# Two orders of the high and low matmuls in a stationary-weight projection

## The chip, the cores and the metric

The kernel runs on one core of one Trainium2 chip. Its time is the device time of one execution in microseconds (us); runs are compared by their medians. The core's engines each work through a queue of their own: TensorE (PE in the profile, its weight loads PEld), VectorE (DVE), ScalarE (ACT), GpSimd (POOL) and SyncE (SP, which issues the DMAs). They wait for each other by semaphores.

## What is computed

A trunk of two layers on 256 tokens of width 2048, all in float32. Layer 0 mixes tokens by differential attention (8 heads, q and k normed, partial rotary), layer 1 by a Mamba-2 state-space mixer (8 groups). Each is followed by an MLP with a squared ReLU of width 8192, and each of the four stages begins with an RMS norm.

```python
for i in range(DEPTH):
    hn = rms_norm(h, mixer_norm[i])
    mix = diff_attention(hn, ...) if i % 2 == 0 else mamba2_mixer(hn, ...)
    h = h + mix
    h = h + sq_relu_mlp(rms_norm(h, mlp_norm[i]), mlp_w1[i], mlp_w2[i])

def sq_relu_mlp(h, w1, w2):
    return jnp.square(jax.nn.relu(h @ w1)) @ w2
```

Nearly all of the work is the projections: q, k, v and o, the mixer's in and out, and the two matrices of each MLP.

## The kernel before

TensorE multiplies in a rounded float32 format (`float32r`), in one pass. To keep float32's precision, both operands are split in two: a high part, which is the value rounded to that format, and a low part, which is the rest. A product is then high x high + high x low + low x high.

Weights come from HBM in blocks of 128 partitions x 1024 columns (`load`, SP's queue, tile `raw`, four buffers). `split_weights` makes the two parts of a block in a tile `w` (four buffers): ACT casts `raw` to the high part `wh` (L158), and DVE subtracts that from `raw` for the low part `wl` (L159).

Two kinds of projection use such blocks. In `sub_block` the weights are stationary: a block holds eight k-tiles of 128 x 128, and each k-tile is loaded into the array and multiplied with 256 tokens of an activation. An activation tile holds its high part and its low part side by side, 256 columns each. So one matmul of the weight's high part takes all 512 columns (L168) and leaves high x high in the left half of a PSUM bank and high x low in the right half. The matmul of the weight's low part takes the activation's high part alone, 256 columns (L172), and adds to the left half. `add_sums` adds the halves later on ACT and DVE (L205, L206). This text calls the 512-column matmul a high one and the 256-column matmul a low one. Before, a block does its eight highs and then its eight lows. Each has its own weight load. q and k (`wide_pair`), the state-space mixer's in-projection (`wide_pair`) and half of each MLP's first matrix (`wide_one`) go this way: 354 blocks in all.

In `token_block` the activations are stationary and the weights move, always 512 columns (L222, L224). `seven` does the other half of the MLP's first matrix by Strassen's scheme, also with 512 columns each (L536 to L538).

Everything smaller (norms, attention scores, rotary, convolution, the scan) is side work. It is written as generators that wait in two queues of `Side`; `side.tick()` lets the first one of each queue go a step further. The projections call `tick` at fixed places: `sub_block` three times in a block, after the fourth high, after the eighth, and after the last low. Where the next activation is not there yet, it ticks until it is. L130 (the norm's mean spread over partitions), L141 (column sums for a norm), L408 and L410 (scores and mask) and L774 (the scan) are matmuls of side work.

A scheduler of the framework then puts the instructions of each engine in order. Mostly it keeps the order of the code, but where it reckons with a wait it moves a later instruction ahead.

Of the kernel before, what the change touches and what calls it, by code (L numbers as in the profile page):

```python
# [20 lines left out]
P = 128  # L21
# [67 lines left out]
def trunk_kernel(ctx: ExitStack, tc: tile.TileContext, x, xt, par, rope, qk, wv, wo, w10, w10s, w20, win, wdt, wout, w11, w11s, w21, out):  # L89
    nc = tc.nc  # L90
    V, S, G, PE = nc.vector, nc.scalar, nc.gpsimd, nc.tensor
# [51 lines left out]
    side = Side()  # L143
# [18 lines left out]
    def sub_block(w, acts, k0, acc, start, stop):  # L162

        wh, wl = w
        for k in range(8):
            while len(acts) <= k0 + k:
                side.tick()
            PE.matmul(acc, lhsT=wh[:, k * P:(k + 1) * P], rhs=acts[k0 + k], start=(start and k == 0), stop=False)  # L168
            if k % 4 == 3:
                side.tick()  # L170
        for k in range(8):
            PE.matmul(acc[:, 0, :], lhsT=wl[:, k * P:(k + 1) * P], rhs=acts[k0 + k][:, 0, :], start=False, stop=(stop and k == 7))  # L172
        side.tick()

    def load(src, n=1):

# [9 lines left out]
    def wide_pair(src, b, acts):  # L186

        pp = [bank() for _ in range(2)]
        for s in range(2):
            raw = [load(src[b + t, s]) for t in range(2)]  # L190
            for t in range(2):
                sub_block(split_weights(raw[t]), acts, 8 * s, pp[t], s == 0, s == 1)
        return pp

    def wide_one(src, b, acts):
        pp = bank()
        raw = [load(src[b, s]) for s in range(2)]
        for s in range(2):
            sub_block(split_weights(raw[s]), acts, 8 * s, pp, s == 0, s == 1)
        return pp  # L200
# [101 lines left out]
    with tc.tile_pool(name="xin", bufs=1) as xp:  # L302
        xf = []
        for j in range(KT // 2):
            f = xp.tile([P, 2, T], F32, name=f"xf{j}")
            nc.sync.dma_start(out=f, in_=x[j])
            xf.append(f)
            if j in (0, 3, 5):
                raw.append(load(qk[len(raw) % 2, len(raw) // 2], 1 if j else 2))
        raw.append(load(qk[1, 1]))  # L310
        for j in range(4):
            nc.scalar.dma_start(out=h[:, :, cols(j)], in_=xt[:, :, cols(j)])
        for s in range(2):
            for j in range(4 * s, 4 * s + 4):
                xs += x_parts(xf[j], j, C_MIX0)
                if j == 4 * s:
                    w = split_weights(raw[2 * s], 1 if s else 2)
            for t in range(2):
                sub_block(w if t == 0 else split_weights(raw[2 * s + 1]), xs, 8 * s, first[t], s == 0, s == 1)
# [656 lines left out]
```

## Time and profile before

| | us |
|---|---|
| median of three runs | 2483.77 |
| the runs | 2481.91 to 2486.58 |
| the profiled execution, its own time | 2483.01 |
| its span, first to last instruction | 2481.3 |
| granted TensorE clock, mean | 1.000 |

The page gives for each engine the time that it was busy. Two groups that the change's neighbours belong to read as follows: the line in the code, the engine and operation, what is written and read, the count, then busy us and the mean ns of one, then idle time of the engine before them and what ended it.

```profile
L159 DVE TENSOR_TENSOR w<-raw,w 128x1024 fp32r<-128x1024 f32 (+1 forms) x739 | 896.3, 1220 | 344.8 <-ACT w L158 341.8
L158 ACT CAST w<-raw 128x1024 fp32r<-128x1024 f32 (+1 forms) x739 | 776.2, 1051 | 594.9 <-PE pp L222 451.6
L172 PEld LDWEIGHTS pp<-act,w 128*128 128x128 f32 x2832 | 384.7, 190 | 28.1 <-issue 1.7
```

A split of a block takes ACT 1051 ns and DVE 1220 ns. A weight load is recorded with 190 ns, beside the matmuls; loads overlap too, which is why 2832 of them are busy for 384.7 us only. The end of a matmul is modelled, so the distance between two starts says more than a duration. In the timeline, equal instructions that follow each other are merged into one row with a count: start, time from the first start to the last end, engine, line. The chain in order of time gives for each piece the time that it holds the end back.

### The profile page before, as it was taken

How to read it: one execution, taken by the hardware profiler on the slowest of the kernel's cores; microseconds unless marked ns; L12 is line 12 of the kernel's file. 1: busy time of each engine (PE TensorE's matmuls, PEld its weight loads, DVE VectorE, ACT ScalarE, POOL GpSimd, SP SyncE). 2: the span in 40 equal slices, each digit the busy share in tenths (PEclk: the TensorE clock that was granted, in tenths of full speed). 3: DMA queues.
4: the chain of work that ended last, by engine and by line, in shares of the span. 5: the costliest groups of instructions: out<-in, count | busy, mean ns of one | idle time of the engine just before them, and what ended most of it. 6: DMA issues, size and time to landing. Idle time of an engine off the chain costs nothing.

```text
span 2481.3 us, 33043 instructions
## 1 busy us (share of the span) xinstructions
PE 2456.4 (99%) x12462; PEld 2070.8 (83%) x12462; DVE 1967.4 (79%) x2558; ACT 1411.4 (57%) x2007; POOL 1.2 (0%) x8
## 2 busy tenths in 40 slices
PE   7999999999999999999999999999999999999999
PEld 6888887888888888888888888888788888888887
DVE  6788879977968949759886887887998696795874
ACT  6666656645545536556776576675565454554553
POOL 0000000000000000000000000000000000000000
PEclk9999999999999999999999999999999999999999
DMA  7445555465565555556555556455555556556554
GB/s 253 159 159 189 169 173 186 176 230 180 198 211 193 202 178 204 170 179 203 197 189 194 172 190 207 159 189 191 192 204 201 182 194 212 190 199 197 186 185 155
DMA packets 131120, 471.21 MB, mean 190 GB/s; under 512 B 14640, under 2 KB 14832, under 8 KB 130960
## 3 DMA queue, kind: packets, MB, share of 16 engines
q1 hardware_dynamic: 127152, 458.28, 54.8%
q10 hardware_dynamic: 3808, 10.81, 1.4%
q8 instruction: 98, 1.61, 0.3%
q14 instruction: 62, 0.51, 0.1%
HBM read 466.88 MB, written 2.16 MB: 189 GB/s over the span
## 4 chain that ended last, share of the span: by engine, by line
PE 96%; DVE 2%; DMA 1%; issue 0%; ACT 0%; ACTq 0%; SPq 0%; DVEq 0%
PE pp L222 27%; PE pp L168 26%; PE pp L172 14%; PE pp L224 13%; PE pp L536 4%; PE pp L537 4%; PE pp L538 4%; DVE w L159 1%; PE aux L774 1%; PE aux L576 1%; PE aux L141 0%; PE aux L408 0%; DMA raw<-in_w11s 0%; DMA h<-in_xt 0%; PE aux L268 0%
## 5 line engine op out<-in xcount | busy, mean ns | idle before, releaser
L159 DVE TENSOR_TENSOR w<-raw,w 128x1024 fp32r<-128x1024 f32 (+1 forms) x739 | 896.3, 1220 | 344.8 <-ACT w L158 341.8
L158 ACT CAST w<-raw 128x1024 fp32r<-128x1024 f32 (+1 forms) x739 | 776.2, 1051 | 594.9 <-PE pp L222 451.6
L222 PE MATMUL pp<-w,act 128*128 128x512 f32 x3072 | 962.7, 392 | 0.0
L168 PE MATMUL pp<-act,w 128*128 128x512 f32 x2832 | 721.7, 394 | 17.2 <-DVE act L250 13.0
L222 PEld LDWEIGHTS pp<-w,act 128*128 128x128 f32 x3072 | 574.7, 188 | 118.7 <-issue 2.1
L168 PEld LDWEIGHTS pp<-act,w 128*128 128x128 f32 x2832 | 511.5, 189 | 114.8 <-ACT w L158 17.9
L224 PE MATMUL pp<-w,act 128*128 128x512 f32 x1536 | 598.5, 390 | 0.0
L172 PEld LDWEIGHTS pp<-act,w 128*128 128x128 f32 x2832 | 384.7, 190 | 28.1 <-issue 1.7
L172 PE MATMUL pp<-act,w 128*128 128x256 f32 x2832 | 398.2, 283 | 0.0
L522 ACT CAST w<-raw 128x1024 fp32r<-128x1024 f32 (+1 forms) x256 | 241.3, 946 | 196.4 <-PE pp L172 111.0
L224 PEld LDWEIGHTS pp<-w,act 128*128 128x128 f32 x1536 | 288.6, 188 | 58.0
L523 DVE TENSOR_TENSOR w<-raw,w 128x1024 fp32r<-128x1024 f32 (+1 forms) x256 | 272.2, 1087 | 41.5 <-ACT w L522 38.5
L536 PE MATMUL pp<-w,sa 128*128 128x512 f32 x256 | 99.9, 390 | 0.0
L537 PE MATMUL pp<-w,sa 128*128 128x512 f32 x256 | 99.8, 390 | 0.0
L538 PE MATMUL pp<-w,sa 128*128 128x512 f32 x256 | 99.6, 389 | 0.0
L529 DVE TENSOR_TENSOR raw<-raw 128x1024 f32<-128x1024 f32 x64 | 78.1, 1221 | 6.8 <-DMA raw<-in_w10s 3.8
L537 PE MATMUL pp<-w,act 128*128 128x512 f32 x192 | 75.2, 391 | 0.0
L536 PE MATMUL pp<-w,act 128*128 128x512 f32 x192 | 75.1, 391 | 0.0
L538 PE MATMUL pp<-w,act 128*128 128x512 f32 x192 | 74.7, 389 | 0.0
L699 DVE SCALAR_TENSOR_TENSOR cy<-u,cwb,cy 128x256 f32<-128x256 f32 x144 | 62.9, 480 | 1.4
L205 ACT COPY relu<-pp 128x256 f32<-128x256 f32 x64 | 23.9, 373 | 63.9 <-PE pp L172 63.9
L536 PEld LDWEIGHTS pp<-w,sa 128*128 128x128 f32 x256 | 48.1, 188 | 10.5
(210 smaller groups left out, 1665.1 us busy)
## 6 DMA issues: line engine op xcount, KB each, us to landing
raw<-in_w SPq DMA_DIRECT2D x384, 512.0 KB, 3.9
raw<-in_win SPq DMA_DIRECT2D x160, 512.0 KB, 3.4
raw<-in_wout SPq DMA_DIRECT2D x64, 512.0 KB, 3.4
raw<-in_qk SPq DMA_DIRECT2D x63, 512.0 KB, 3.4
raw<-in_w10s SPq DMA_DIRECT2D x32, 768.0 KB, 4.4
raw<-in_w11s SPq DMA_DIRECT2D x32, 768.0 KB, 4.4
raw<-in_wv SPq DMA_DIRECT2D x32, 512.0 KB, 4.1
raw<-in_wo SPq DMA_DIRECT2D x32, 512.0 KB, 3.8
```

The source lines that it names most:

```text
L158: S.copy(out=wh[:, s], in_=raw[:, s])
L159: V.tensor_tensor(out=wl[:, s], in0=raw[:, s], in1=wh[:, s].bitcast(F32), op=ALU.subtract)
L168: PE.matmul(acc, lhsT=wh[:, k * P:(k + 1) * P], rhs=acts[k0 + k], start=(start and k == 0), stop=False)
L172: PE.matmul(acc[:, 0, :], lhsT=wl[:, k * P:(k + 1) * P], rhs=acts[k0 + k][:, 0, :], start=False, stop=(stop and k == 7))
L222: PE.matmul(pp[t], lhsT=act[:, 0, tok], rhs=m, start=(s + i + k == 0), stop=(s == n - 1 and i + k == 2))
L224: PE.matmul(pp[t], lhsT=act[:, 1, tok], rhs=m, start=False, stop=False)
L522: S.copy(out=w[:, 0], in_=r[:, a:a + n, :])
L523: V.tensor_tensor(out=w[:, 1], in0=r[:, a:a + n, :], in1=w[:, 0].bitcast(F32), op=ALU.subtract)
L529: V.tensor_tensor(out=r[:, 3:5, :], in0=r[:, 0:2, :], in1=bc(r[:, 6, :], 2), op=ALU.subtract)
L536: PE.matmul(pp[n], lhsT=ah, rhs=wh, start=start, stop=False)
L537: PE.matmul(pp[n], lhsT=al, rhs=wh, start=False, stop=False)
L538: PE.matmul(pp[n], lhsT=ah, rhs=wl, start=False, stop=stop)
```

## The change

In `sub_block` the second loop is gone. Each low matmul now follows the high one of the same k-tile. The three ticks stand after the third, the sixth and the eighth pair. The number of matmuls, loads and ticks is the same, and so are tiles, buffers and DMAs.

```diff
         for k in range(8):
             while len(acts) <= k0 + k:
                 side.tick()
-            PE.matmul(acc, lhsT=wh[:, k * P:(k + 1) * P], rhs=acts[k0 + k], start=(start and k == 0), stop=False)
-            if k % 4 == 3:
+            kk = slice(k * P, (k + 1) * P)
+            PE.matmul(acc, lhsT=wh[:, kk], rhs=acts[k0 + k], start=(start and k == 0), stop=False)
+            PE.matmul(acc[:, 0, :], lhsT=wl[:, kk], rhs=acts[k0 + k][:, 0, :], start=False, stop=(stop and k == 7))
+            if k in (2, 5, 7):
                 side.tick()
-        for k in range(8):
-            PE.matmul(acc[:, 0, :], lhsT=wl[:, k * P:(k + 1) * P], rhs=acts[k0 + k][:, 0, :], start=False, stop=(stop and k == 7))
-        side.tick()
```

The lines behind it move up by one, so that L168 and L172 are now L169 and L170, and L222 is L221.

The scheduler's order moves with the code. The first place is on TensorE at about 33 us, in the k projection of the first head, where the side work's L130 stands; pp, act and w are the PSUM bank, the activation tile and the weight block, with their numbers. Before:

```order
L168 MATMUL pp_281<-act_180,w_349 128x512 x2
L168 MATMUL pp_281<-act_188,w_349 128x512 x2
L130 MATMUL aux_321<-dge_322,ones_r_73 128x128
L130 MATMUL aux_321<-dge_325,ones_r_73 128x128
L168 MATMUL pp_281<-act_193,w_349 128x512 x2
L168 MATMUL pp_281<-act_198,w_349 128x512 x2
L172 MATMUL pp_281<-act_180,w_349 128x256 x2
```

And now:

```order
L170 MATMUL pp_282<-act_140,w_308 128x256
L169 MATMUL pp_281<-act_180,w_349 128x512
L130 MATMUL aux_325<-dge_326,ones_r_73 128x128
L130 MATMUL aux_325<-dge_329,ones_r_73 128x128
L170 MATMUL pp_281<-act_180,w_349 128x256
L169 MATMUL pp_281<-act_180,w_349 128x512
```

L130 stood behind four highs of the block and now stands behind its first one. The second place is on TensorE at about 105 us, in the k projection of the second head; w_1012 and w_1041 are its last two blocks, w_1069 the first block of the v projection behind it. It comes three times, at every second head. Before:

```order
L168 MATMUL pp_956<-act_198,w_1012 128x512 x2
L168 MATMUL pp_957<-act_180,w_1041 128x512 x2
L168 MATMUL pp_957<-act_188,w_1041 128x512
L172 MATMUL pp_956<-act_180,w_1012 128x256
L141 MATMUL aux1_1005<-sqr_975,ones_r_73 128x512
L172 MATMUL pp_956<-act_180,w_1012 128x256
```

And now:

```order
L169 MATMUL pp_956<-act_180,w_1012 128x512
L169 MATMUL pp_957<-act_180,w_1041 128x512
L221 MATMUL pp_1065<-w_1069,act_120 128x512
L223 MATMUL pp_1065<-w_1069,act_120 128x512
L407 MATMUL aux_1080<-qkn_580 128x128
L409 LDWEIGHTS ident_b_258
L409 MATMUL aux_1080<-mask_b_265,ident_b_258 128x128
L407 MATMUL aux_1080<-qkn_580 128x256
L221 MATMUL pp_1066<-w_1069,act_120 128x512
L223 MATMUL pp_1066<-w_1069,act_120 128x512
```

Before, eight highs of w_1012 and three of w_1041 stood ahead of the first low one; now one high of each, and behind them six matmuls of the v projection, the scores of a head and one L141 (the rows go on with those) ahead of the first low one. Elsewhere highs and lows simply alternate. The orders of SP and POOL are the same as before; DVE and ACT keep the order of their splits, with a few norm and score instructions of attention standing some places earlier or later.

## The prediction

> **What bounds the kernel now.** I read the page first, from the top: busy shares, the granted clock, the chain that ended last, then the groups of the two lines that the change touches.
>
> ```profile
> span 2481.3 us, 33043 instructions
> PE 2456.4 (99%) x12462; PEld 2070.8 (83%) x12462; DVE 1967.4 (79%) x2558; ACT 1411.4 (57%) x2007; POOL 1.2 (0%) x8
> PEclk9999999999999999999999999999999999999999
> PE 96%; DVE 2%; DMA 1%; issue 0%; ACT 0%; ACTq 0%; SPq 0%; DVEq 0%
> L168 PE MATMUL pp<-act,w 128*128 128x512 f32 x2832 | 721.7, 394 | 17.2 <-DVE act L250 13.0
> L172 PE MATMUL pp<-act,w 128*128 128x256 f32 x2832 | 398.2, 283 | 0.0
> ```
>
> TensorE is busy 99% of the span at full granted clock and makes up 96% of the chain. So the end moves by whatever the matmul stream gains or loses per instruction, and by almost nothing else. The change adds and removes no instruction. It reorders 2832 high matmuls (512 columns, L168) and 2832 low ones (256 columns, L172), 8 and 8 to a block, 2832/8 = 354 blocks. The durations 394 and 283 ns are of no use for the sum, since matmuls overlap in the pipeline. What counts is the time from one start to the next, and the chain in order of time gives it. Here is a stretch of the state-space layer, where a token block (L222) ends and three stationary-weight blocks follow; the columns are start, time on the chain, what:
>
> ```profile
> 1511.21 1.81 PE pp L168 x8
> 1513.02 0.95 PE pp L172 x8
> 1513.98 1.84 PE pp L168 x8
> 1515.82 0.95 PE pp L172 x8
> 1516.77 1.84 PE pp L168 x8
> ```
>
> Eight highs that follow 512-column matmuls take 1.81 us, 226 ns each. Eight highs that follow a run of lows take 1.84, 230 each: 0.03 us more for the run. Eight lows take 0.95, 119 each. A block with lows ahead of it costs 1.84 + 0.95 = 2.79 us, 349 ns a pair. A token or Strassen matmul that follows lows pays the 0.03 too, as the timeline of the first MLP shows right behind a low run (the first, sixth and eleventh matmul):
>
> ```profile
> 1002.99 0.40 PE L536 MATMUL pp<-w,act 128*128 128x512 f32 x1
> ...
> 1004.15 0.39 PE L538 MATMUL pp<-w,sa 128*128 128x512 f32 x1
> ...
> 1005.28 0.39 PE L537 MATMUL pp<-w,sa 128*128 128x512 f32 x1
> ```
>
> The first five steps take 1.16 us, the next five 1.13. So I charge every block with 2.79: 354 x 2.79 = 988 us of the span, 40%.
>
> **The change part by part: the pitch.** In the new order every high stands between two lows and every low between two highs. The trace has the two edges, but hardly that neighbourhood. High to low costs one high, low to high one low. What each costs depends on what ran ahead. The sum goes by the slopes above: a high ahead of which no run of lows has built up is 226 to 227 ns (1.81/8; 1.13/5 = 226), a low 119 to 120 (0.95/8). That is 227 + 120 = 347 ns a pair, 2 less than 349, so 2832 x 2 ns = 5.7 us less. The assumption is that the 0.03 us is a price of a *run* of lows, of which there is none left.
>
> Its bounds come from the two nearest neighbourhoods. One: two single 256-column matmuls (L141, sums for a norm) between 512-column ones in attention:
>
> ```profile
> 210.63 0.40 PE L141 MATMUL aux<-sor,ones_r 128*128 128x256 f32 x2
> 210.86 0.39 PE L222 MATMUL pp<-w,act 128*128 128x512 f32 x1
> 211.09 0.39 PE L224 MATMUL pp<-w,act 128*128 128x512 f32 x1
> ```
>
> The two take 0.23 us, some 115 ns each, and the matmul behind them 0.23: nothing is paid back. With 113 to 115 for a low and 227 for a high a pair is 340 to 342, 7 to 9 ns less: 20 to 26 us less. Two: one high alone among lows, which the scheduler made where the MLPs and the state-space layer start:
>
> ```profile
> 422.48 0.40 PE L168 MATMUL pp<-act,w 128*128 128x512 f32 x1
> 422.71 1.46 PE L172 MATMUL pp<-act,w 128*128 128x256 f32 x11
> ...
> 1114.33 0.41 PE L168 MATMUL pp<-act,w 128*128 128x512 f32 x1
> 1114.58 1.60 PE L172 MATMUL pp<-act,w 128*128 128x256 f32 x12
> ...
> 1797.21 0.39 PE L168 MATMUL pp<-act,w 128*128 128x512 f32 x1
> 1797.44 1.24 PE L172 MATMUL pp<-act,w 128*128 128x256 f32 x9
> ```
>
> That high takes 0.23, 0.25 and 0.23 us, a mean of 237 ns. With 117 to 119 for the low behind it a pair is 354 to 356: 5 to 7 ns more, 14 to 20 us more. The ends are far apart; I take 347, which the many rows give, and keep both ends for the range.
>
> On weight loads: each matmul has its own, before and after, and a low at 119 ns in a run of eight shows that a load can be had every 119 ns. In the new order a load falls beside each high and each low in turn, so no load is asked for faster than the trace shows. The Trainium skill, TensorE: Matmul & The Clock Gate, section on the back-to-back issue gap, gives N/2.4 + 2.5 ns, thus 216 and 109 ns and 325 a pair, whatever the order. The trace has 227 and 119, 10 more for each, so the measurement decides the size.
>
> **The wait for the low part.** Before, a block's first low stands behind eight highs, 1.81 us after its first high; now it is the second matmul. DVE makes the low part (L159) behind ACT's high part (L158), so DVE may now be late by up to 1.6 us more than it could be. Behind a waiting load stands all of TensorE's queue. What is waited for now:
>
> ```profile
> PEld pp L168 <- ACT w L158: 17.9, 4, 12.5
> PEld pp L172 <- DVE w L159: 0.6, 3, 0.2
> ```
>
> Two places matter. At the heads with a token block behind them (three times, first at 105 us) DVE is behind:
>
> ```profile
> 105.50 2.68 PE L168 MATMUL pp<-act,w 128*128 128x512 f32 x11
> ...
> 106.69 2.34 DVE L159 TENSOR_TENSOR w<-raw,w 128x1024 fp32r<-128x1024 f32 x2
> ```
>
> The first of these two low parts is done at 106.69 + 2.34/2 = 107.9, 2.4 us after the block's first high. Left as written, TensorE would stand for 2.1 us, three times 6.4 us. But the scheduler's order (shown above) puts two highs, six token matmuls, the scores of a head and a sum there: 8 x 0.227 + about 0.9 for the scores (an estimate from L408 and L410's rows in the group list, five matmuls) = 2.7 us. That covers 2.1, so I cost it at 0; uncovered it is +6.4. The other side's tightest steady place, in the state-space layer:
>
> ```profile
> 1213.71 1.22 DVE L159 TENSOR_TENSOR w<-raw,w 128x1024 fp32r<-128x1024 f32 x1
> ...
> 1216.12 1.09 PE L168 MATMUL pp<-act,w 128*128 128x512 f32 x4
> ```
>
> The low part is there at 1214.93, 1.2 us ahead of the block's first high, so nothing waits. Four buffers of w let ACT and DVE run ahead; their release, the last low, does not move, nor does any row of SP's or POOL's queue.
>
> **The start.** The block at 27.22 us gets its low part at 28.04, so TensorE now stands for some 0.6 us. And L130 (two matmuls on DVE's dge) is hoisted from behind four highs to behind one:
>
> ```profile
> 26.81 1.23 DVE L159 TENSOR_TENSOR w<-raw,w 128x1024 fp32r<-128x1024 f32 x1 [1.14 <-ACT w L158]
> ...
> 33.31 0.48 DVE L129 TENSOR_SCALAR dge<-ident,em 128x128 f32<-128x128 f32 x2
> ...
> 33.74 0.63 PE L130 MATMUL aux<-dge,ones_r 128*128 128x128 f32 x4
> ```
>
> dge is done at 33.79 either way. By then four highs of that block were through before, one or two now: two or three highs are late, 3 x 0.23 = +0.7 us. The stand at 27 us and what the first block gains (its lows no longer wait for the last activation) end in the same wait, so they are not added. The starts of the MLPs and of the state-space layer are left at 0, by 1 us either way.
>
> **Sum.** 2483.0 (the profiled execution: span 2481.3 and 1.7 around it; the median of the runs shown is 0.8 above) - 5.7 + 0.7 = 2478 us, 0.2% less.
>
> **The rivals.** *Lows are cheap among highs* (340 to 344 a pair): for it speaks 210.63; against it, those were two lows in a long row of 512-column matmuls, not every second one. 2483.7 - 14 to - 26: 2458 to 2469. *The order does not matter*: each matmul keeps the mean time of its kind, 349 a pair, and the 0.03 us is no price of runs. The Trainium skill, TensorE: Matmul & The Clock Gate, section on the back-to-back issue gap, has in its formula no term for order and would give this too. Then 2483.7, so 2479 to 2488. *The high pays after every low* (slower): the 0.03 us is a recovery that starts anew behind each low, with 234 to 237 ns for every high and 117 to 120 for the low, 351 to 356 a pair. For it speak the three single highs and the 1.84 against 1.81; against it the pair at 210.63, which cost nothing. It decides from the point where a pair passes 349 ns: 2483.7 + 5 to + 19, 2489 to 2503. The attention heads' 6.4 us would come on top of any case.
>
> **How the numbers follow.** Forecast, 346 to 348 a pair: 0.40, with 2475 to 2481. Cheap lows 0.20, order indifferent 0.14, slower 0.26. A measurement of this kernel tells some 0.2%, 5 us, from no change. Of the forecast 0.23 lies beyond that, 0.17 within. Faster: 0.23 + 0.20 + 0.02 = 0.45; the same: 0.17 + 0.10 + 0.01 = 0.28; slower: 0.25 + 0.02 = 0.27. The range must take in most of both neighbours, so 2460 to 2498; the likeliest case's own is 2475 to 2481.
>
> **What would show it.** In the chain in order of time a pair's two rows sum to 0.347 us, and the span between two side matmuls divided by its pairs gives the same. 0.340 or 0.354 there names the rival. In the waits of TensorE's loads, a row of the low line on DVE's w of more than 2 us would show that the hoisted work does not cover. L130 should start at 33.8 us. The forecast is wrong if highs behind single lows take 234 ns.

## The result, and the profile after

| | before | after |
|---|---|---|
| median, us (6 runs of each, side by side) | 2482.43 | 2493.83 |
| the runs, us | 2481.34 to 2486.58 | 2491.08 to 2496.58 |
| ratio after/before, 95% interval | | 1.0048 [1.0038, 1.0058] |
| span of the profiled execution, us | 2481.3 | 2489.4 |

The change makes the kernel 0.5% slower. The time lies inside the range that was given, on the other side of no change: the forecast was 2478.

The page of after, the same lines as shown of before:

```profile
span 2489.4 us, 33038 instructions
PE 2467.0 (99%) x12462; PEld 2070.8 (83%) x12462; DVE 1969.6 (79%) x2558; ACT 1409.1 (57%) x2007; POOL 1.2 (0%) x8
PEclk9999999999999999999999999999999999999999
PE 96%; DVE 2%; DMA 1%; issue 0%; ACT 0%; ACTq 0%; SPq 0%; DVEq 0%
L169 PE MATMUL pp<-act,w 128*128 128x512 f32 x2832 | 1013.9, 401 | 16.3 <-DVE act L249 12.1
L170 PE MATMUL pp<-act,w 128*128 128x256 f32 x2832 | 794.5, 281 | 0.0
```

The picture is the old one: TensorE is busy 99% at full clock, 96% of the chain is its own, the counts are equal, the idle time ahead of the highs is 16.3 us against 17.2. No new wait has come in. The busy sums of the two groups (1013.9 and 794.5, before 721.7 and 398.2) say nothing: a merged run of overlapping matmuls counts once, single ones count with their overlap.

So the stream itself is longer. The chain in order of time, in the state-space layer, where a token block ends and pairs follow; the columns are start, time on the chain, what:

```profile
1515.60 0.23 PE pp L169
1515.82 0.12 PE pp L170
1515.94 0.23 PE pp L169
1516.17 0.12 PE pp L170
1516.29 0.24 PE pp L169
...
1517.00 0.23 PE pp L169
...
1518.06 0.23 PE pp L169
```

From 1515.94 to 1517.00 three pairs pass, and from there to 1518.06 three more: 1.06 us for three, 353.3 ns a pair. The trace holds starts in whole nanoseconds; by them the stretch repeats every three pairs: high 236, low 113, high 232, low 118, high 241, low 120, in all 1060 (in the MLPs 233 and 117 stand for 232 and 118). Two streams of one kind stand against this: 512-column matmuls in a row start every 226.7 ns (227, 227, 226), lows in a row every 120. A pair without any loss would be 226.7 + 120 = 346.7. The cycle loses 20 ns in every three pairs.

The starts also give the account of the whole difference. The time from each matmul's start to the next one's, summed by the kind of the first, in us:

| | before | after | difference |
|---|---|---|---|
| highs | 659.4 | 676.0 | +16.6 |
| lows | 340.5 | 334.3 | -6.2 |
| all other matmuls | 1464.2 | 1462.3 | -1.9 |
| start of the first matmul | 12.48 | 12.15 | -0.3 |

Together +8.2, and the span grew by 8.1. The medians lie 11.4 apart, since after's profiled execution is the fastest of its six; that remainder isn't explained by one trace.

One thing in the same trace did not fit a fixed price of alternation. Behind a piece of side work (L130) at 1118 us the chain reads:

```profile
1118.14 0.44 PE aux L130 x4
1118.59 0.23 PE pp L169
1118.82 0.12 PE pp L170
1118.94 0.23 PE pp L169
1119.17 0.12 PE pp L170
1119.29 0.23 PE pp L169
...
1121.71 0.23 PE pp L169
```

From 1118.94 to 1121.71 eight pairs pass in 2.77 us, 346 ns each: the forecast's price, in the same order of the same instructions. By the starts this is a cycle of two pairs, 350 and 343 ns to within 1 ns (233 + 117, 231 + 112), with no loss at all, and it holds for 78 pairs. Of 228 stretches of eight pairs with a low ahead of them, 19 lie within 7 ns of the lossless 2773 ns, and 203 lie 40 to 60 ns above it. Before, 208 of 209 blocks of 8 + 8 with a low ahead of them lie 15 to 21 ns above it.

### The profile page after: what moved, and what is told of

Its sections match the earlier page's. It is cut to its first block, busy times and chain, and to the rows that moved or that the text cites. A ratio compares the mean times of both kernels' runs of the same rounds, so it can differ in the third digit from the quotient of the medians.

```text
span 2489.4 us, 33038 instructions
## 1 busy us (share of the span) xinstructions
PE 2467.0 (99%) x12462; PEld 2070.8 (83%) x12462; DVE 1969.6 (79%) x2558; ACT 1409.1 (57%) x2007; POOL 1.2 (0%) x8
## 4 chain that ended last, share of the span: by engine, by line
PE 96%; DVE 2%; DMA 1%; issue 0%; ACT 0%; ACTq 0%; SPq 0%; DVEq 0%
PE pp L169 27%; PE pp L221 26%; PE pp L170 14%; PE pp L223 13%; PE pp L536 4%; PE pp L535 4%; PE pp L537 4%; DVE w L159 1%; PE aux L773 1%; PE aux L575 1%; PE aux L407 0%; PE aux L141 0%; DMA raw<-in_w11s 0%; DMA h<-in_xt 0%; PE aux L267 0%
## 5 line engine op out<-in xcount | busy, mean ns | idle before, releaser
L169 PE MATMUL pp<-act,w 128*128 128x512 f32 x2832 | 1013.9, 401 | 16.3 <-DVE act L249 12.1
L221 PE MATMUL pp<-w,act 128*128 128x512 f32 x3072 | 963.3, 392 | 0.0
L170 PE MATMUL pp<-act,w 128*128 128x256 f32 x2832 | 794.5, 281 | 0.0
L221 PEld LDWEIGHTS pp<-w,act 128*128 128x128 f32 x3072 | 574.6, 188 | 119.1 <-issue 2.1
L169 PEld LDWEIGHTS pp<-act,w 128*128 128x128 f32 x2832 | 532.9, 188 | 148.0 <-ACT w L158 17.5
L170 PEld LDWEIGHTS pp<-act,w 128*128 128x128 f32 x2832 | 536.2, 189 | 5.1 <-DVE w L159 1.4
```

Source lines behind the costliest of these rows:

```text
L169: PE.matmul(acc, lhsT=wh[:, kk], rhs=acts[k0 + k], start=(start and k == 0), stop=False)
L170: PE.matmul(acc[:, 0, :], lhsT=wl[:, kk], rhs=acts[k0 + k][:, 0, :], start=False, stop=(stop and k == 7))
L221: PE.matmul(pp[t], lhsT=act[:, 0, tok], rhs=m, start=(s + i + k == 0), stop=(s == n - 1 and i + k == 2))
```

## The experiments

All are single edits of the changed kernel, unless something else is said. They ran in five groups, each beside the kernel before (medians 2482.03, 2481.47, 2483.18, 2482.24, 2482.07), so the ratios are what can be compared. Lines of the edits differ by a few from the change's: the high is L167, L168 or L169, the low L168 to L174.

### Where the low's result goes, and what it reads

First suspicion: the low adds to the bank address that the high ahead has just written, or reads the activation that the high has just read. The first edit lets the low add to the other half of the bank.

```diff
-            PE.matmul(acc[:, 0, :], lhsT=wl[:, kk], rhs=acts[k0 + k][:, 0, :], start=False, stop=(stop and k == 7))
+            PE.matmul(acc[:, 1, :], lhsT=wl[:, kk], rhs=acts[k0 + k][:, 0, :], start=False, stop=(stop and k == 7))
```

> The pairs as in the changed kernel, but each low matmul adds to the right half of the PSUM bank instead of the left (the halves are added later, so the output is the same sum). Clean pairs of the changed kernel take 352 ns on average (high 235, low 117). If the extra 5 to 6 ns over 347 come from the low and the next high writing the same addresses, the pair here falls to 347 or changes by more than 2 ns, and the time by 6 us or more. If they come from the alternation of widths or of weights on the array, 352 stays and the time is within 5 us of the changed kernel, about 2493 us.

Measured: 2491.10 us, 1.0037 [1.0023, 1.0050]; highs 235.4 ns, lows 116.9 (means without the waits; the change has 235.4 and 116.8), the same cycle of three pairs to the nanosecond. Which half of the bank the low adds to plays no part. The high writes both halves, so this run alone doesn't rule out the bank; the low with 512 columns, further down, adds to the whole bank behind each high and loses nothing.

The second edit sets the low of k-tile k-1 behind the high of k-tile k, so that neighbours share neither weights nor activation:

```diff
-            PE.matmul(acc[:, 0, :], lhsT=wl[:, kk], rhs=acts[k0 + k][:, 0, :], start=False, stop=(stop and k == 7))
+            for j in ([k - 1] if k else []) + ([7] if k == 7 else []):
+                PE.matmul(acc[:, 0, :], lhsT=wl[:, j * P:(j + 1) * P], rhs=acts[k0 + j][:, 0, :], start=False, stop=(stop and j == 7))
```

> Each low follows the high of the next k-tile, so that no low reads the activation that the high ahead of it has just read; only the last low of a block does. If reading the same activation twice in a row costs the extra, the pair falls to about 347 ns and the time to about 2478 us. If the alternation itself costs it, 352 ns stays, and the time is about 2493 us.

Measured: 2488.62 us, 1.0027 [1.0016, 1.0037]; highs 234.4, lows 117.3. Within a block it is the old cycle again (236, 113, 233, 117, 241, 120); only at the block ends, where two lows and two highs meet, do the starts differ. Sharing an activation isn't the cause.

### How many stand together

Groups of two (high, high, low, low) and of four. The lows' own line of the change is gone, and the first tick moves from behind the third high to behind the fourth:

```diff
             PE.matmul(acc, lhsT=wh[:, k * P:(k + 1) * P], rhs=acts[k0 + k], start=(start and k == 0), stop=False)
-            PE.matmul(acc[:, 0, :], lhsT=wl[:, kk], rhs=acts[k0 + k][:, 0, :], start=False, stop=(stop and k == 7))
-            if k in (2, 5, 7):
+            if k % 2 == 1:          # groups of four: k % 4 == 3
+                for j in range(k - 1, k + 1):          # groups of four: range(k - 3, k + 1)
+                    PE.matmul(acc[:, 0, :], lhsT=wl[:, j * P:(j + 1) * P], rhs=acts[k0 + j][:, 0, :], start=False, stop=(stop and j == 7))
+            if k in (3, 5, 7):
                 side.tick()
```

> Two highs, then two lows. Theory recovery (a high pays after every low, and several highs are needed to get over it; the steps in a run of highs behind lows are 234, 236, 228, 232, 231, 227 in the trace of before): highs 234 and 236, lows 113 to 119, thus 351 ns a pair, as bad as one and one; time about 2490 us. Theory edge (each change from low to high costs the 5.5 ns of a pair once, wherever): half as many edges, 349.5 ns a pair, about 2486 us.

> Four highs, then four lows. Theory recovery: highs 234, 236, 228, 232, lows 117, 118, 119, 120, thus 351 ns a pair, about 2489 us, and no better than groups of two. Theory edge: a quarter of the edges, 348 ns a pair, about 2481 us.

Measured: groups of two 2479.55 us, 0.9986 [0.9977, 0.9995], less than either theory asked for; groups of four 2487.03, 1.0021 [1.0012, 1.0031]. The chain of groups of two:

```profile
1510.95 0.47 PE pp L168 x2
1511.42 0.23 PE pp L171 x2
1511.65 0.46 PE pp L168 x2
1512.12 0.23 PE pp L171 x2
1512.35 0.47 PE pp L168 x2
```

Four pairs from 1510.95 to 1512.35, 1.40 us; by the starts 1393.3 ns, 348.3 a pair (233, 236, 116, 112, 233, 230, 114, 119). Here the second high of a group costs as much as the first. The timeline of groups of four (start, first start to last end, line):

```profile
809.36 1.09 PE L168 MATMUL pp<-act,w 128*128 128x512 f32 x4
810.29 0.63 PE L171 MATMUL pp<-act,w 128*128 128x256 f32 x4
810.76 1.09 PE L168 MATMUL pp<-act,w 128*128 128x512 f32 x4
```

Four pairs in 1.40 as well, by the starts 1403.3, 350.8 a pair. Fewer changes of width and yet dearer than groups of two: no price for each return from low to high can give that.

### Runs of sixteen, and the ticks

Both are edits of the kernel before. The first puts sixteen highs of two blocks ahead of their sixteen lows; `highs` and `lows` are the two loops of the old `sub_block`. The second keeps the order of 8 + 8 and puts the ticks behind the fifth high, the second low and the last low. The first, in `wide_pair`:

```diff
+            w = []
             for t in range(2):
-                sub_block(split_weights(raw[t]), acts, 8 * s, pp[t], s == 0, s == 1)
+                w.append(split_weights(raw[t]))
+                highs(w[t], acts, 8 * s, pp[t], s == 0)
+            for t in range(2):
+                lows(w[t], acts, 8 * s, pp[t], s == 1)
```

> The other way: sixteen highs of two blocks, then their sixteen lows. In the trace of before eight highs behind lows take 27 ns more than eight behind 512-column matmuls, and a run of lows starts 8 ns cheap. Per run that is 19 ns; with half as many runs 177 x 19 ns = 3.4 us less than before, 2479 us, if the price is paid once a run. If it is paid in proportion to the lows (as after one and one it is not), the time stays at 2482 us. The low parts are needed later, so no wait is added.

> Eight highs and eight lows as before, but the three ticks stand where they come in time in the changed kernel (after the fifth high, the second low, the last low). If the shifted side work has a part in the 11 us, the time moves from 2482 us by 2 us or more; if the order of the matmuls is all, it stays within 2 us.

Measured: 2482.27 us, 1.0002 [0.9993, 1.0010], and 2481.26 us, 1.0001 [0.9992, 1.0010]. Moving the ticks does nothing to the time. The chain of the runs of sixteen:

```profile
1509.15 3.63 PE pp L167 x16
1512.78 1.91 PE pp L174 x16
1514.69 3.65 PE pp L167 x16
```

Sixteen highs behind 512-column matmuls take 3.63, behind lows 3.65: the 0.02 to 0.03 us that the prediction saw are paid once behind a run of sixteen lows, as behind eight. They lie in the first five highs (234, 235, 229, 232, 231 and then 227). The 3.4 us that half as many runs should have saved didn't come: by the starts the highs take 4.1 us less than before, but the lows 4.0 more.

### The width of the low

With 512, 384 and 448 columns for the low (parts of low x low are added that the reference leaves out, so these are dearer by design):

```diff
-            PE.matmul(acc[:, 0, :], lhsT=wl[:, kk], rhs=acts[k0 + k][:, 0, :], start=False, stop=(stop and k == 7))
+            PE.matmul(acc.rearrange("p a b -> p (a b)")[:, 0:384], lhsT=wl[:, kk], rhs=acts[k0 + k].rearrange("p a b -> p (a b)")[:, 0:384], start=False, stop=(stop and k == 7))
```

> One and one, but each low matmul takes all 512 columns (low x low is added in the right half, which no other kernel here computes). The work grows by 2832 times 227 - 117 = 110 ns, 311 us. Theory short cover (a matmul's weight load is issued when the matmul ahead of it starts; behind a low it has only 113 to 120 ns, the record of a load is 188 ns, and the high pays for it): every load now has 227 ns, so both kinds take 227 ns flat, 454 ns a pair. Theory weights (alternating between the two weight parts costs, whatever the width): highs stay above 230 ns.

> One and one, low matmuls of 384 columns (low x low is added for half of the tokens). With the fixed 13.3 ns above the streaming time that highs and lows alone show (226.7 and 120 ns) a low takes 173.3 ns. Theory short cover: a load behind a low has 173 ns, nearly its 188, so the high falls to 227 to 229 ns and the pair to about 401 ns. Theory width change (any change of width between neighbours costs 3 ns): the pair stays 5 to 6 ns above 400, highs at 233 and more. Time about 2482 + 2832 x (401 - 349) = 2629 us, or 2644 us.

> Pairs as in the change, but the low part has 448 columns instead of 256 (it adds the low weight part to 192 columns of the low activation part too, which the reference leaves out). Theory 'short cover' (a high pays when its own load had less than the 188 ns of a load record to run beside the matmul ahead): the low now takes about 200 ns, so the highs go flat at 227 and a pair takes 427 ns. Theory 'unlike widths' (a high pays because its neighbours have another width, whatever the cover): highs stay at 230 ns or more, a pair takes 430 or more.

Measured: 2780.66, 2654.05 and 2729.76 us, one execution each; 2654 is above what either theory gave for 384 columns. The chain of the low with 512 columns, then of the one with 448:

```profile
1539.81 0.23 PE pp L168
1540.03 0.23 PE pp L169
1540.26 0.23 PE pp L168
...
1542.07 0.23 PE pp L168
```

```profile
1700.14 0.24 PE pp L168
1700.37 0.20 PE pp L169
1700.58 0.23 PE pp L168
...
1701.45 0.24 PE pp L168
```

Equal widths are flat: 227.1 for the high, 227.2 for the low in the mean, and 226.7 for both in long stretches, though each still loads its own weights and the two weight parts alternate. With 448 columns three pairs take 1.31 us, 437.8 a pair by the starts, with highs of 236, 233, 233 and lows of 200, 208, 203. The two flat streams (226.7 ns for 512 columns, 120 for 256) differ by 0.417 ns a column, so a low of 448 without loss is estimated at 200 and the pair at 426.7: it loses 11. The low of 384 gives 406.7 in some long stretches and 413.3 in others, where the same estimate gives 400. So a lasting loss is seen only where two widths alternate, and it does not go when the low gives the next load 200 ns of cover, more than the 188 to 190 of a recorded load. The theory of a short cover falls.

A change of width alone isn't what makes the loss, though, as the starts of the kernel before show. At 118.91 us two sums for a norm (L141) stand in a row of token matmuls, all of them with 512 columns. The stream had run at 227; from the first sum on it goes 233, 232, 231, 231, 235, 229, 232, 231 and then 227 again, 41 ns lost in eight, and three more places like it lose the same. And the two 256-column sums at 210.63, between 512-column matmuls, go 116, 118 and then 227: two changes of width and no loss, at five places. So an equal-width stream can be thrown out of its rhythm too, but it comes back within eight matmuls or so.

### Groups of three, and groups of two again

> Order of groups 3, 3 and 2: three highs, their three lows, three more highs and lows, then two and two; ticks behind the third, sixth and eighth high. The computation is whole. Theory 'the price hangs on the cycle that a pattern falls into': no smooth law, the mean pair lies somewhere between the 348.3 ns of groups of two and the 353.3 ns of pairs; nothing finer is promised. Theory 'every return from low to high costs the same': returns per block 8 (pairs), 4 (groups of two), 3 (here), 2 (groups of four), 1 (before), so the time would fall between groups of two and of four, 2479.6 to 2487.0 us, about 2483. Theory 'a group's first high is cheap, its later ones are dear': the highs in a steady stretch go cheap, dear, dear. Rival 'groups of two were a fortune of one call': e9 is not above e10.

> The order high, high, low, low once more, unchanged from e3_groups2, to see whether the version that came out ahead of both kernels does so again on another chip job. If the cycle of 1393.3 ns for four pairs is what sets it: 2478 to 2481 us, ratio 0.998 to 0.9995 of the kernel before. If it was the chip of that job: a ratio of 1.000 or above.

Measured: groups of 3, 3 and 2 at 2482.72 us, 0.9997 [0.9988, 1.0006], 349.5 a pair in long stretches; groups of two again at 2480.82, 0.9992 [0.9983, 1.0000], with its cycle unchanged. The 2482.7 fits the 2483 of an equal price for each return, but groups of four had already broken that rule. In order of group size a pair takes 353.3 (one), 348.3 (two), 349.5 (three), 350.8 (four), 349.2 (eight).

### The entry of a stretch

What was left is the finding in after's own trace: one order, two cycles. If the place where a stretch begins chooses the cycle, a nudge there must change everything behind it. The nudge makes two neighbouring pairs trade places inside (high, high, low, low) once, in the first block of a bank's sum, and leaves the rest alternating:

```diff
+        at = 2 if start else 8          # e13: 0, e14: 1, e15: 2 in every block
...
-            PE.matmul(acc[:, 0, :], lhsT=wl[:, kk], rhs=acts[k0 + k][:, 0, :], start=False, stop=(stop and k == 7))
-            if k in (2, 5, 7):
+            for j in ([] if k == at else [at, k] if k == at + 1 else [k]):
+                PE.matmul(acc[:, 0, :], lhsT=wl[:, j * P:(j + 1) * P], rhs=acts[k0 + j][:, 0, :], start=False, stop=(stop and j == 7))
+            if k in (3, 5, 7):
```

> The change, but in the first block of every projection's bank (the block that starts its sum) the third and fourth pairs trade places inside: high 2, high 3, low 2, low 3; all else alternates. The computation is whole. The trace of the change holds two repeating cycles of the same alternation: three pairs in 1060 ns (340, 350, 361 to 350; mean 353.3) in nearly all places, and two pairs in 693 ns (350 and 343; mean 346.7) in others, among them 78 pairs from 1118 us on and 10 pairs from 1803 us on, just behind a place where two highs and two lows stood together in the sequence 117, 241, 237, 117, 118, 233. Theory 'two cycles, chosen where a stretch begins': this nudge copies that sequence behind 512-column matmuls, so the MLP's stretches of 16 pairs (352.5 ns now) go to about 347.5 a pair behind the nudge, and with some of the mixer's the time falls by 5 to 14 us, to 2478 to 2488. Rival 'pairs cost 353 in steady work, and the 347 stretches stand only behind waits': it stays at 2488 to 2494.

> As e12_nudge2, but the nudge stands at the first two pairs: high 0, high 1, low 0, low 1. The computation is whole. Theory 'two cycles, chosen where a stretch begins': which place of the cycle the nudge meets decides, so this one may do what e12 does or nothing; in either case all stretches of the MLP, which begin behind 512-column matmuls, go the same way: 347 or 353 ns a pair. Rival 'pairs cost 353': 2488 to 2494 here and in e12.

> As e12_nudge2, but the nudge stands at the second and third pairs: high 1, high 2, low 1, low 2. The computation is whole. Theory 'two cycles': again 347 or 353 ns a pair in all stretches of the MLP alike, and at least one of the three nudges gives 347. Rival 'pairs cost 353': 2488 to 2494 in all three.

> As e12_nudge2, but in every block and not only in those that start a sum. The computation is whole. Theory 'two cycles': the second nudge meets the stream in the cycle that the first has left it in, so it may throw it out again; if it does, the time lies above e12's; if the good cycle holds through a nudge, it lies at or below e12's, down to 2476 us, since the mixer's later blocks are nudged too. Rival 'pairs cost 353': 2486 to 2494.

Measured, with the mean pair in the 60 undisturbed stretches of 16 pairs in the MLPs, which begin behind 512-column matmuls:

| | MLP pair, ns | median, us | ratio to before |
|---|---|---|---|
| the change | 352.5 | 2493.83 | 1.0048 [1.0038, 1.0058] |
| nudge at pairs 0, 1 (e13) | 352.3 | 2487.25 | 1.0020 [1.0009, 1.0030] |
| nudge at pairs 1, 2 (e14) | 346.7 | 2483.38 | 1.0005 [0.9995, 1.0014] |
| nudge at pairs 2, 3 (e12) | 347.7 | 2483.78 | 1.0008 [0.9999, 1.0017] |
| e12's nudge in every block (e15) | 349.4 | 2487.79 | 1.0024 [1.0014, 1.0033] |

The same MLP stretch in the chain with the nudge at pairs 0 and 1, then with that at pairs 1 and 2:

```profile
805.73 0.45 PE pp L169 x2
806.18 0.23 PE pp L171 x2
806.41 0.23 PE pp L169
...
807.47 0.23 PE pp L169
...
808.53 0.23 PE pp L169
```

```profile
806.82 0.23 PE pp L169
807.05 0.12 PE pp L171
807.16 0.47 PE pp L169 x2
807.63 0.23 PE pp L171 x2
807.86 0.23 PE pp L169
...
809.24 0.23 PE pp L169
...
810.63 0.23 PE pp L169
```

Behind the first nudge three pairs take 1.06 us, twice in a row: the lossy cycle. Behind the second, four pairs take 1.38 and eight 2.77: the lossless one. The two kernels differ in the places of two lows in sixteen pairs (high, high, low, low, high, low against high, low, high, high, low, low); their ticks are the same. The rival, a price of 353 for alternation in steady work, falls: it asked for 2488 to 2494 in the first three, and e12 and e14 lie 4 to 5 us below that. e13, without effect in the MLP, is still below the change, because its nudges changed the mixer: the stretches of 139 to 140 pairs there take 348.3 ns a pair, against 353.3 in the change. A second nudge throws the stream out of the good cycle again: in e15 the MLP's mean rises from 347.7 to 349.4, and the time from 2483.8 to 2487.8 (a time that the rival would allow too). The starts show it in each of these stretches: the cycle is lossless behind the first nudge and goes 241, 120, 236, 113, 233, 117 behind the second. The same is to be seen in e14's mixer, where a stretch holds several nudged blocks: by the starts it runs lossless from the first nudge on, the second turns it to 241, 120, 235, 114, 232, 118, and the third turns it back.

### The best of them

The MLP's blocks with the nudge of e14, all others in groups of two:

```diff
+            if pairs:
+                js = [] if start and k == 1 else [1, 2] if start and k == 2 else [k]
+            else:
+                js = [k - 1, k] if k % 2 else []
...
-            sub_block(split_weights(raw[s]), acts, 8 * s, pp, s == 0, s == 1)
+            sub_block(split_weights(raw[s]), acts, 8 * s, pp, s == 0, s == 1, True)
```

> What the cycles suggest as the best of the orders tried: the MLP's stretches (1024 pairs, behind 512-column matmuls) alternate with the nudge of e14_nudge1 in their first block, all other blocks go in groups of two as in e3_groups2. The computation is whole. Theory 'two cycles, chosen where a stretch begins': the MLP's pairs take 346.7 ns against 347.7 in e3 and 352.5 in the change, so this is 1.0 us below groups of two: about 2478 to 2480, ratio 0.998 to 0.9995 of before. Rival 'e14's 346.7 came from its mixer's state, too': MLP pairs at 348 or more, time at or above that of groups of two, 2480 to 2484.

Measured: 2480.20 us, 0.9993 [0.9984, 1.0002]; the MLP's pairs take 346.7 ns, as expected, which the rival excluded; the time stands just above the 2478 to 2480 that were expected, the ratio inside its range. So the cycle can be chosen for one stage alone. The microsecond that this is worth against groups of two can't be told apart in the time. Against the change both versions are clearly faster; against the kernel before, groups of two are ahead by about 0.1% in two groups of runs (0.9986 and 0.9992), which is as much as can be measured here. The pairs explain only a part of that: by the starts all highs and lows together take 999.9 us before, 999.2 and 999.0 in the two runs of groups of two, and 997.9 here.

## Why the prediction was wrong

- **The frame held.** TensorE's stream sets the end; the account by starts gives +8.2 us for a span that grew by 8.1.
- **The step that failed** is the pitch of the sum: "The assumption is that the 0.03 us is a price of a *run* of lows, of which there is none left", hence 347 ns a pair and -5.7 us. Measured: 352 a pair in the mean without the waits (349 before), highs and lows together +10.4 us. The 0.03 us isn't a price that goes away with the runs: where single lows stand between highs, the stream settles in a cycle that loses 20 ns in every three pairs, or, in 19 of its 228 stretches of eight pairs, in one that loses nothing. 347 is what both streams give without any loss. That the time still lies inside the stated range is owed to the slower rival, for which the range was drawn up to 2498.
- **The rows that misled.** The pair of 256-column matmuls at 210.63 did cost nothing (116, 118 and then 227 by the starts), but it was side work with a weight tile of its own. In the new order a first low behind 512-column matmuls comes early too (113 ns), yet the next high takes 232 or 233. The three single highs of 0.23 to 0.25 us were the better witnesses; the rival that they speak for was given a chance of 0.26.
- **The slower rival** (351 to 356 a pair, 2489 to 2503) had the size right. Its mechanism, a recovery that starts anew behind each low, holds only in the lossy cycle: in the lossless one every high stands behind a low too, and the pair is 346.7. The steady rows of before showed one cycle, that of 8 + 8; a new order has a cycle of its own, and none of those rows told which.
- **Order does not matter** fell by the same runs: the orders tried, all of the same instructions, lie between 2479.6 and 2493.8 us. The Trainium skill, TensorE: Matmul & The Clock Gate, section on the back-to-back issue gap, has a formula in which the gap depends on the column count alone; the steady equal-width streams agree with that form (226.7 and 120 ns, each 11 above its figure), the mixed ones do not.
- **The wait for the low part** at 0 was right. The waits of the weight loads in after:

```profile
PEld pp L169 <- ACT w L158: 17.5, 4, 12.1
PEld pp L170 <- DVE w L159: 1.4, 4, 0.4
```

  Columns are the total, the count and the longest. The lows wait 0.8 us more in all than before, never over 0.4 at once; the hoisted token matmuls and scores cover the attention heads.
- **The start** was off by little. L130 was to start at 33.8 us. DVE's dge (L129) and L130 in after, and the first token matmul in after, then in before:

```profile
32.93 0.48 DVE L129 TENSOR_SCALAR dge<-ident,em 128x128 f32<-128x128 f32 x2
33.27 0.71 PE L130 MATMUL aux<-dge,ones_r 128*128 128x128 f32 x4
39.62 0.40 PE L221 MATMUL pp<-w,act 128*128 128x512 f32 x1
```

```profile
39.35 0.40 PE L222 MATMUL pp<-w,act 128*128 128x512 f32 x1
```

  L130 starts at 33.27, since DVE itself was 0.38 earlier (L129 at 32.93, before 33.31), which the forecast had taken as fixed. The token block begins 0.27 us later than before, where +0.7 was charged.

## What to carry to other kernels

Where matmuls of unlike widths follow each other without a gap, a change of their order has a price of its own, up to 2% of a pair here, that the rows of the old order didn't show; measure the new order, and look at the starts over several periods, since a stream can settle in different cycles. If an order comes out dear, try groups of two, or one swap where the stretch begins, before giving the idea up. A pair of rows beside another kind of work is no witness for a steady stream.

## What the runs showed of the hardware that was not expected

- Steady streams of equal width are flat (226.7 ns for 512 columns, 120 for 256), for 512 columns even where the weight parts alternate. Two sums of another kind in such a row cost it 41 ns over the next eight matmuls, without any change of width. A mix of widths settles in cycles that lose 0 ns (two pairs in 693), 20 ns in three pairs (1060), 6.7 in four (groups of two, 1393), 17 in four (groups of four, 1403) or 20 in eight (8 + 8, 2793).
- One order can run in two cycles, 353.3 and 346.7 ns a pair, for as long as it is left alone (139 and 78 pairs seen). Swapping one low and one high where the stretch begins chooses between them; a second swap undoes it. With a low of 384 columns two cycles are seen as well, 406.7 and 413.3.
- What in TensorE makes the loss stays open. The half of the bank, the shared activation, the weight part, the ticks and the cover of the next load were each changed and are not it; no run put neighbouring highs and lows in different banks or changed the number of weight loads, and none tried another data type.
